# Both products of a squared-ReLU MLP by Strassen's seven products on halves, after a FoX attention layer

## The chip, the cores and the metric

The kernel runs on one core of a Trainium2 chip. The metric is the device time of one execution in microseconds (us): the median of several runs, 2275.89 us for the kernel before (three runs, 2275.84 to 2275.94). The profiled execution is another run of the same program.

## The reference

One decoder layer on 512 tokens (S) of width 2048 (D), all in float32. Attention has 16 heads of 128; the MLP is 8192 wide.

```python
h = rmsnorm(x, g[0])
proj = h @ w_in                                  # q, k, v and one forget gate per head
cum = cumsum(log_sigmoid(f_pre + b_f))           # per head
logits = q @ k.T * dh**-0.5 + cum[i] - cum[j]    # causal
h = softmax(logits) @ v @ w_out
x = x + rmsnorm(h, g[1])
h = square(relu(rmsnorm(x, g[2]) @ w1)) @ w2     # w1 [2048, 8192], w2 [8192, 2048]
x = x + rmsnorm(h, g[3])
```

## The kernel before

Every float32 operand is carried in two parts of TensorE's fp32r type: `h`, the value rounded by a cast on ScalarE (ACT), and `l`, the remainder, a subtraction on VectorE (DVE). `mm3` (L69 to L73) makes each product by three matmuls: h·h, h·l and l·h. A 512 KB block of weights comes by SyncE (SP) DMA into one of three `raw` buffers, ACT casts it (L65) and DVE subtracts (L66); four places of `whi` and `wlo` hold the blocks that TensorE (PE) works on.

The stages follow one another: values, queries and keys, per-head attention, output projection `py` in four chunks of 512 columns, first residual, MLP, last norm and residual. The output projection's last chunk goes by halves of the tokens (tiles 0, 1 and then 2, 3), so that the residual and the transposes of the first half (`turn_pair`) stand between PE's work on the second half, and those of the second half between PE's first MLP products (`first_chunk`, L520). All sixteen 256 KB tiles `xt` of the layer's input are loaded by GpSimd (POOL) well ahead (`load_x`, L412). `residual` (L440) scales the projected tile by the norm's factor and adds `xt`, for some tiles on POOL (L444, L445), for others on DVE (L447). The second norm's factor is a row `r2row` that is multiplied in after the first MLP product (L505), so nothing waits for it before PE starts.

The MLP goes in 16 chunks of four tiles of its width. `w1_chunk` makes four hidden tiles of 128 x 512 in PSUM, each over 16 tiles of D, with moving operands of 512 columns (the tokens); DVE takes the relu, ACT squares and casts, DVE makes the low part, and all stays in SBUF. `w2_chunk` of the chunk before follows: for each of four column chunks, four PSUM sums `po` of 128 tokens x 512 columns over the chunk's four hidden tiles, which DVE adds to sixteen accumulators `acc` in SBUF (L568). Chunks of the first and the second product alternate, so that each one's evacuation lies beside the other's matmuls. The last chunk's second product goes by tiles of tokens (`pz`, L609 to L640), each followed by its norm, residual and store.

Engines work in order, each through its own queue; an instruction that waits holds all behind it on that engine. The order is that of the code as a scheduler places it.

## Time and profile before

| what | value |
|---|---|
| median of three runs | 2275.89 us |
| profiled execution, first to last instruction (span) | 2273.5 us |
| PE busy, matmuls | 2257.2 us, 9978 |
| DVE, ACT, POOL busy | 1002.4, 667.5, 130.0 us |
| DMA, hardware queue and POOL's software queue | 226.65 MB and 6.33 MB |
| mean granted PE clock | 0.998 of 2.4 GHz |

Times are us from the span's start, durations of one instruction ns where so marked. A PE instruction's own duration overlaps its neighbours', because matmuls are pipelined: what one costs in a run of many is the distance from start to start, which the time-ordered view shows. "Idle before" is how long the engine stood still in front of the instructions of a row, with the instruction that ended most of it. A DMA row's last number is the median from issue to landing.

### The profile page before, as it was taken

What the parts mean: (1) busy time and instruction counts of PE and PEld (TensorE: products, weight loads), DVE (VectorE), ACT (ScalarE), POOL (GpSimd) and SP (SyncE); (2) the same over time, 40 slices, a digit from 0 to 9 for tenths busy, and PEclk for the clock granted to TensorE, in tenths of its full rate; (3) what the DMA queues carried; (4) which work ended last, traced back from release to release, by engine and by line L of the source; (5) the groups of instructions that cost most, each with busy time, mean ns of one, the idle gap of its engine ahead of it and who ended that gap; (6) DMA issues with size and microseconds to landing.
All of it is one profiled execution on the core that took longest, in us unless ns stands there. A gap on an engine that the chain in (4) does not pass through costs nothing.

```text
span 2273.5 us, 24519 instructions
## 1 busy us (share of the span) xinstructions
PE 2257.2 (99%) x9978; PEld 1826.0 (80%) x9978; DVE 1002.4 (44%) x1312; ACT 667.5 (29%) x981; POOL 130.0 (6%) x147
## 2 busy tenths in 40 slices
PE   9999999999999999999999999999999999999998
PEld 7788888888888888888888888888888888888886
DVE  9553452544542383433334334334334343343455
ACT  4433332333432363222222222222222222222232
POOL 8000000000010030000000000000000000000002
PEclk9999999999999999999999999999999999999999
DMA  5322222222243362222222222322222222322243
GB/s 173 117 90 86 92 88 93 88 89 92 85 153 116 122 211 94 93 93 98 95 95 93 93 93 93 94 96 96 94 93 93 93 94 94 98 95 93 93 146 123
DMA packets 70720, 234.55 MB, mean 103 GB/s; under 512 B 8128, under 2 KB 8512, under 8 KB 70352
## 3 DMA queue, kind: packets, MB, share of 16 engines
q1 hardware_dynamic: 68832, 226.65, 30.8%
q0 software_dynamic: 1632, 6.33, 0.8%
q8 instruction: 78, 1.28, 0.2%
q14 instruction: 34, 0.28, 0.0%
q10 hardware_dynamic: 144, 0.02, 0.0%
HBM read 224.54 MB, written 8.42 MB: 102 GB/s over the span
## 4 chain that ended last, share of the span: by engine, by line
PE 95%; DVE 3%; DMA 1%; issue 1%; ACT 1%; SPq 0%; DVEq 0%; ACTq 0%
PE ph L73 10%; PE ph L71 10%; PE ph L72 10%; PE po L72 10%; PE po L73 10%; PE po L71 10%; PE pk L71 3%; PE pk L72 3%; PE pq L72 3%; PE pq L73 3%; PE pk L73 3%; PE pq L71 3%; PE py L71 2%; PE py L73 2%; PE py L72 2%; PE pv L71 2%
## 5 line engine op out<-in xcount | busy, mean ns | idle before, releaser
L71 PE MATMUL ph<-acth,whi_a 128*128 128x512 f32 (+1 forms) x1056 | 412.1, 390 | 0.0
L72 PE MATMUL ph<-actl,whi_a 128*128 128x512 f32 (+1 forms) x1056 | 411.4, 390 | 0.0
L73 PE MATMUL ph<-acth,wlo_a 128*128 128x512 f32 (+1 forms) x1056 | 411.3, 390 | 0.0
L72 PE MATMUL po<-wlo_b,hh 128*128 128x512 f32 x960 | 379.3, 395 | 0.0
L71 PE MATMUL po<-whi_b,hh 128*128 128x512 f32 x960 | 379.2, 395 | 0.0
L73 PE MATMUL po<-whi_b,hl 128*128 128x512 f32 x960 | 379.2, 395 | 0.0
L65 ACT CAST whi_a<-raw_a 128x1024 fp32r<-128x1024 f32 x128 | 134.6, 1052 | 523.5 <-PE ph L72 268.5
L66 DVE TENSOR_TENSOR wlo_a<-raw_a,whi_a 128x1024 fp32r<-128x1024 f32 x128 | 157.2, 1228 | 265.0 <-ACT whi_a L65 264.8
L65 ACT CAST whi_b<-raw_b 128x1024 fp32r<-128x1024 f32 x120 | 126.0, 1050 | 496.0 <-PE po L73 257.6
L66 DVE TENSOR_TENSOR wlo_b<-raw_b,whi_b 128x1024 fp32r<-128x1024 f32 x120 | 147.1, 1225 | 253.1 <-ACT whi_b L65 253.1
L72 PEld LDWEIGHTS ph<-actl,whi_a 128*128 128x128 f32 x1056 | 199.0, 188 | 45.6
L73 PEld LDWEIGHTS ph<-acth,wlo_a 128*128 128x128 f32 x1056 | 199.0, 188 | 45.5
L71 PEld LDWEIGHTS ph<-acth,whi_a 128*128 128x128 f32 x1056 | 198.9, 188 | 45.4
L71 PEld LDWEIGHTS po<-whi_b,hh 128*128 128x128 f32 x960 | 180.0, 188 | 44.1
L72 PEld LDWEIGHTS po<-wlo_b,hh 128*128 128x128 f32 x960 | 180.0, 187 | 44.0
L73 PEld LDWEIGHTS po<-whi_b,hl 128*128 128x128 f32 x960 | 179.9, 187 | 44.0
L568 DVE TENSOR_TENSOR acc<-po,acc 128x512 f32<-128x512 f32 x224 | 149.3, 686 | 78.7 <-PE po L73 78.5
L505 DVE SCALAR_TENSOR_TENSOR a<-ph,r2row 128x512 f32<-128x512 f32 x64 | 44.2, 691 | 216.6 <-PE ph L73 216.5
L73 PE MATMUL pv<-whi_v,actl 128*128 128x512 f32 x256 | 102.0, 398 | 3.0 <-DVE actl L191 3.0
L72 PE MATMUL pv<-wlo_v,acth 128*128 128x512 f32 x256 | 102.2, 399 | 0.6 <-DVE wlo_v L66 0.2
L71 PE MATMUL pv<-whi_v,acth 128*128 128x512 f32 x256 | 102.4, 402 | 0.2 <-ACT whi_v L65 0.2
L71 PE MATMUL py<-whi_o,acth 128*128 128x512 f32 x256 | 102.6, 401 | 0.0
(171 smaller groups left out, 2868.1 us busy)
## 6 DMA issues: line engine op xcount, KB each, us to landing
raw_a<-in_w SPq DMA_DIRECT2D x128, 512.0 KB, 3.7
raw_b<-in_w SPq DMA_DIRECT2D x120, 512.0 KB, 3.5
raw_o<-in_wo SPq DMA_DIRECT2D x40, 512.0 KB, 3.5
raw_q<-in_wq SPq DMA_DIRECT2D x32, 512.0 KB, 3.7
raw_k<-in_wk SPq DMA_DIRECT2D x32, 512.0 KB, 3.8
raw_v<-in_wv SPq DMA_DIRECT2D x24, 512.0 KB, 3.5
xr<-in_xT SPq DMA_DIRECT2D x16, 256.0 KB, 4.0
raw_v<-in_wv SPq DMA_DIRECT2D x16, 256.0 KB, 4.1
```

The costliest lines, as they stand in the source:

```text
L65: nc.scalar.copy(hi[:, c], raw[:, c])
L66: nc.vector.tensor_tensor(out=lo[:, c], in0=raw[:, c], in1=f32(hi[:, c]), op=ALU.subtract)
L71: nc.tensor.matmul(o, a[0], b[0], start=start, stop=False)
L72: nc.tensor.matmul(o, a[0], b[1], start=False, stop=False)
L73: nc.tensor.matmul(o, a[1], b[0], start=False, stop=stop)
L505: nc.vector.scalar_tensor_tensor(out=a, in0=ps, scalar=0.0, in1=r2row, op0=ALU.max, op1=ALU.mult)
L568: nc.vector.tensor_tensor(out=acc[t, c], in0=po[t], in1=acc[t, c], op=ALU.add)
```

## The change

Seven products of quarter-size blocks replace eight in both MLP products, for 30 of the 32 pairs of hidden tiles. A pair is 256 hidden columns. In the first product the halves are of the inner dimension D, of the pair's hidden columns (128 and 128) and of the tokens (256 and 256); in the second they are of the pair's hidden tiles, of the tokens and of the 2048 output columns, taken 256 + 256 at a time in four column pairs `cp`. Every matmul of both now has 256 moving columns.

- Weights (`load_seven`): one SP DMA of 512 KB brings four blocks of 256 columns, DVE makes the four sums that the scheme needs (`t8_combine`), ACT casts the seven operands (1792 columns in one instruction), DVE subtracts (1792). There are two places for the split operands and three `raw` buffers.
- First product: the normed input's seven combinations are made once (`turn`, `mix`, `split_mix`) and stay in SBUF. The first 512 hidden columns are done plainly, by halves of the tokens (`plain`), while those are made. Then each pair is 168 matmuls into four PSUM banks; `evac_seven` combines the seven sums, takes relu and square, and POOL stores the hidden tile to DRAM (`hd`).
- Second product: `load_h` brings a pair back from DRAM by POOL's DMA, combines and splits it. Five chunks of six pairs; in each, four column pairs; in each of these, seven PSUM sums of 128 x 512 over six pairs. ACT copies the sums to four `st` buffers and POOL's DMA writes them to DRAM (`md`), plainly in the first chunk and with addition in the other four. The two MLP products no longer alternate.
- At the end `gather` reads `md` back and combines seven sums into four for each column pair; the last two pairs of hidden tiles are added as before (`pz`).
- The second norm's factor is now applied to the residual tiles (`norm2`) ahead of the transposes. The input tiles have two buffers for each half of the tokens' work, loaded by POOL inside `residual`. Head outputs go to DRAM and come back for the output projection (`od`).

```diff
@@ helpers in place of the [128, 1024] blocks of the MLP
+    AOF = [1, 6, 0, 4, 3, 5, 2]
+    def t8_combine(z):
+        nc.vector.tensor_tensor(out=z[:, 4:6], in0=z[:, 1:3], in1=z[:, 0:1].to_broadcast([P, 2, 256]), op=ALU.add)
+        nc.vector.scalar_tensor_tensor(out=z[:, 6], in0=z[:, 4], scalar=-1.0, in1=z[:, 2], op0=ALU.mult, op1=ALU.subtract)
+        nc.vector.tensor_tensor(out=z[:, 7], in0=z[:, 3], in1=z[:, 6], op=ALU.subtract)
+    def split7(z, at):
+        hi, lo = slots(at, 7), slots(at + SLOT, 7)
+        nc.scalar.copy(hi, z[:, 1:8])
+        nc.vector.tensor_tensor(out=lo, in0=z[:, 1:8], in1=f32(hi), op=ALU.subtract)
+        return hi, lo
+    def load_seven(src, name):
+        raw = raw_tile(f"raw_{name}").rearrange("p (n c) -> p n c", c=256)
+        nc.sync.dma_start(raw[:, 0:4], src)
+        t8_combine(raw)
+        tplace[0] += 1
+        return split7(raw, WBASE + tplace[0] % 2 * 2 * SLOT)
...
@@ residual, second norm, mixed inputs
-                y = vpool.tile([P, 512], F32, tag="yg", name=f"yg_{c}_{t}", bufs=16)
...
-            xx = mp.tile([P, 512], F32, tag="xt", name=f"xt_{c}_{t}", bufs=16)
...
+        def residual(hf, c, on_pool):
+            for t in halves[hf]:
+                xx = tr.tile([P, 512], F32, tag="xt", name=f"xt_{c}_{t}", bufs=2)
+                cs = slice(c * 512, (c + 1) * 512)
+                nc.gpsimd.dma_start(xx, x[t * P:(t + 1) * P, cs])
+                y, r = yg[t, c], r1[:, t:t + 1]
+                if on_pool:
+                    nc.gpsimd.tensor_scalar(out=y, in0=y, scalar1=r, scalar2=None, op0=ALU.mult)
+                    nc.gpsimd.tensor_tensor(out=y, in0=y, in1=xx, op=ALU.add)
+                else:
+                    nc.vector.scalar_tensor_tensor(out=y, in0=y, scalar=r, in1=xx, op0=ALU.mult, op1=ALU.add)
+                nc.sync.dma_start(x2d[:, t, cs], y)
+                nc.scalar.activation(xx, y, AF.Square, accum_out=ssx[:, t, c:c + 1])
+        def norm2(hf):
...
+            for c in (0, 2, 1, 3):
+                for t in halves[hf]:
+                    nc.scalar.activation(yg[t, c], yg[t, c], AF.Copy, scale=r2[:, t:t + 1])
+        def turn(hf, p):
...
+        def mix(p, x4):
...
+            nc.vector.tensor_tensor(out=x4[:, 0:512], in0=f32(opr[:, at:at + 512]), in1=f32(opr[:, at + 512:at + 1024]), op=ALU.add)
+            nc.vector.tensor_tensor(out=m[:, 0:2], in0=z[:, 1:3], in1=z[:, 3:4].to_broadcast([P, 2, 256]), op=ALU.subtract)
+            nc.vector.tensor_tensor(out=m[:, 2], in0=m[:, 1], in1=z[:, 1], op=ALU.add)
+            nc.vector.tensor_tensor(out=m[:, 3], in0=z[:, 0], in1=m[:, 2], op=ALU.subtract)
+            return m4
...
+        for hf in range(2):
+            for kb in range(8):
+                out_unit(py, NC - 1, kb, halves[hf])
+                if hf == 1:
+                    if kb == 0:
+                        norm1(0)
+                        for c in range(NC):
+                            residual(0, c, c % 2 == 1)
+                        norm2(0)
+                    if kb >= 6:
+                        for p in range(4 * kb - 24, 4 * kb - 20):
+                            turn(0, p)
+            evac_y(py, NC - 1, halves[hf])
...
+        def plain(hf, p):
+            w = load_split(w1p[p], f"a{hf}_{p}")
+            cols = slice(256 * hf, 256 * (hf + 1))
...
+        for p in range(8):
+            plain(0, p)
+            if p == 0:
+                norm1(1)
+                for c in range(NC):
+                    residual(1, c, c == 1)
+                norm2(1)
+        for p in range(8):
+            plain(1, p)
+            split_mix(p, m4[p])
+            if p + 2 < 8:
+                m4[p + 2] = mix(p + 2, x4[p + 2])
+            if p + 3 < 8:
+                x4[p + 3] = turn(1, p + 3)
@@ first product
-    def w1_tile(ci, f):
-        ps = psum_acc(f"ph_{ci}_{f}")
-        for hb in range(2):
-            w1_mm(ps, w1_block(ci, f, hb), hb)
-        return ps
...
+        def square(h4, src, n):
+            if src is not None:
+                nc.scalar.activation(h4, src, AF.Relu)
+            nc.scalar.activation(h4, h4, AF.Square)
+            nc.gpsimd.dma_start(hd[n], h4)
...
+        def evac_seven(b, n):
...
+            nc.scalar.copy(s1[:, 0], b[0][:, 0:256])
+            nc.vector.tensor_tensor(out=ev[:, 0:6:5], in0=two[1], in1=s1.to_broadcast([P, 2, 256]), op=ALU.add)
+            nc.vector.tensor_tensor(out=ev[:, 1], in0=b[2][:, 0:256], in1=ev[:, 0], op=ALU.add)
+            nc.vector.scalar_tensor_tensor(out=ev[:, 2:7:4], in0=two[0][:, 1:2].to_broadcast([P, 2, 256]), scalar=-1.0, in1=ev[:, 0:2],
+                                           op0=ALU.mult, op1=ALU.subtract)
+            nc.vector.tensor_tensor(out=ev[:, 3:5], in0=two[3], in1=ev[:, 1:3], op=ALU.add)
+            square(h4, ev[:, 3:7].rearrange("p n c -> p (n c)"), n)
+        for n in range(2, NPAIR):
+            b = [(psum_acc if n % 2 else psum_att)(f"ps_{n}_{i}") for i in range(4)]
+            for g in range(4):
+                w = load_seven(w1s[n - 2, g], f"a{n}_{g}")
+                for j in range(7):
+                    bi, part = WHERE[j]
+                    for kk in range(2):
+                        p = 2 * g + kk
+                        mm3b(b[bi][:, part * 256:(part + 1) * 256], [zz[:, j, kk * P:(kk + 1) * P] for zz in w], xop(p, AOF[j]),
+                             p == 0 and FIRST[bi] == j, p == 7)
+            evac_seven(b, n)
@@ second product
-    def w2_chunk(ci, hs):
...
-                    nc.vector.tensor_tensor(out=acc[t, c], in0=po[t], in1=acc[t, c], op=ALU.add)
...
+    def load_h(pool, n):
+        h8 = pool.tile([P, 8, 256], F32, tag="h8", name=f"h8_{n}", bufs=2)
+        nc.gpsimd.dma_start(h8[:, 0:4], hd[n].rearrange("p (n c) -> p n c", c=256))
+        nc.vector.tensor_tensor(out=h8[:, 4:6], in0=h8[:, 2:4], in1=h8[:, 0:1].to_broadcast([P, 2, 256]), op=ALU.subtract)
+        nc.vector.tensor_tensor(out=h8[:, 6], in0=h8[:, 5], in1=h8[:, 2], op=ALU.add)
+        nc.vector.tensor_tensor(out=h8[:, 7], in0=h8[:, 1], in1=h8[:, 6], op=ALU.subtract)
+        return split7(h8, n % NRING * 2 * SLOT)
...
+        for n in range(3):
+            want(n)
+        for ci in range(NCHUNK):
+            n0 = ci * CHUNK
+            for cp in range(4):
+                po = []
+                for k in range(CHUNK):
+                    n = n0 + k
+                    w = load_seven(w2s[n, cp], f"b{n}_{cp}")
+                    for j in range(7):
+                        if k == 0:
+                            po.append(psum(f"po_{ci}_{cp}_{j}"))
+                        for t in range(2):
+                            mm3b(po[j][:, t * 256:(t + 1) * 256], [zz[:, AOF[j], t * P:(t + 1) * P] for zz in hops[n]], [zz[:, j] for zz in w],
+                                 k == 0 and t == 0, k == CHUNK - 1)
+                    if ci == 0 and cp == 0 and k < 3:
+                        want(n + 3)
+                    elif ci > 0 and cp == 0 and k in (0, 2):
+                        want(n0 + 4 + k // 2)
+                    if cp in (1, 2) and k == 2:
+                        want(n0 + CHUNK + cp - 1)
+                    if cp == 3 and k in (2, 4):
+                        want(n0 + CHUNK + 1 + k // 2)
...
+                for j in range(7):
+                    st = w2pool.tile([P, 512], F32, tag="st", name=f"st_{ci}_{cp}_{j}", bufs=4)
+                    nc.scalar.copy(st, po[j])
+                    if ci == 0:
+                        nc.gpsimd.dma_start(md[cp, :, j], st)
+                    else:
+                        nc.gpsimd.dma_start(md[cp, :, j], st, accum_op=ALU.add)
...
@@ end
+        def gather(cp):
+            ma = raw_tile(f"ma_{cp}").rearrange("p (n c) -> p n c", c=512)
+            mb = raw_tile(f"mb_{cp}").rearrange("p (n c) -> p n c", c=512)
+            nc.sync.dma_start(ma, md[cp, :, 0:4])
+            nc.sync.dma_start(mb[:, 0:3], md[cp, :, 4:7])
...
+            nc.vector.tensor_tensor(out=p6, in0=p1, in1=p6, op=ALU.add)
+            nc.vector.tensor_tensor(out=y(0, 0), in0=two(p1), in1=two(p2), op=ALU.add)
+            nc.vector.tensor_tensor(out=p3, in0=p3, in1=p5, op=ALU.subtract)
+            nc.vector.tensor_tensor(out=y(0, 1), in0=two(p3), in1=two(p6), op=ALU.subtract)
+            nc.vector.tensor_tensor(out=p7, in0=p6, in1=p7, op=ALU.add)
+            nc.vector.tensor_tensor(out=y(1, 0), in0=two(p7), in1=two(p4), op=ALU.add)
+            nc.vector.scalar_tensor_tensor(out=y(1, 1), in0=two(p5), scalar=-1.0, in1=two(p7), op0=ALU.mult, op1=ALU.subtract)
```

In POOL's queue the first half's residual stood like this before: sixteen loads of the input far ahead, then only arithmetic (`yg` the projected tile, `xt` the input tile, `r1` the first norm's factor; names end in a running number).

```order
L415 DMA xt_3_0_5867<-in_x 128x512
L415 DMA xt_3_1_5869<-in_x 128x512
L415 DMA xt_3_2_5871<-in_x 128x512
L415 DMA xt_3_3_5873<-in_x 128x512
L444 TENSOR_SCALAR yg_2_0_5853<-yg_2_0_5853,r1_5875 128x512
L444 TENSOR_SCALAR yg_2_1_5857<-yg_2_1_5857,r1_5875 128x512
L445 TENSOR_TENSOR xt_2_0_5599<-yg_2_0_5853,xt_2_0_5599 128x512
L445 TENSOR_TENSOR xt_2_1_5601<-yg_2_1_5857,xt_2_1_5601 128x512
L444 TENSOR_SCALAR yg_3_0_6030<-yg_3_0_6030,r1_5875 128x512
L444 TENSOR_SCALAR yg_3_1_6034<-yg_3_1_6034,r1_5875 128x512
L445 TENSOR_TENSOR xt_3_0_5867<-yg_3_0_6030,xt_3_0_5867 128x512
L445 TENSOR_TENSOR xt_3_1_5869<-yg_3_1_6034,xt_3_1_5869 128x512
```

Now the loads stand among the arithmetic, each pair of buffers behind its last reader:

```order
L507 TENSOR_SCALAR yg_0_0_4960<-yg_0_0_4960,r1_4948 128x512
L507 TENSOR_SCALAR yg_1_0_4962<-yg_1_0_4962,r1_4948 128x512
L507 TENSOR_SCALAR yg_0_1_4961<-yg_0_1_4961,r1_4948 128x512
L507 TENSOR_SCALAR yg_1_1_4963<-yg_1_1_4963,r1_4948 128x512
L504 DMA xt_1_0_5625<-in_x 128x512
L504 DMA xt_1_1_5631<-in_x 128x512
L508 TENSOR_TENSOR yg_0_0_4960<-yg_0_0_4960,xt_1_0_5625 128x512
L504 DMA xt_2_0_5637<-in_x 128x512
L508 TENSOR_TENSOR yg_1_0_4962<-yg_1_0_4962,xt_1_1_5631 128x512
L504 DMA xt_2_1_5642<-in_x 128x512
L504 DMA xt_3_0_5647<-in_x 128x512
L508 TENSOR_TENSOR yg_0_1_4961<-yg_0_1_4961,xt_3_0_5647 128x512
```

All four scalings of the tiles done on POOL now come ahead of the third load, and each addition behind the load of its own tile.

On ACT, at the end of one column pair and the start of the next in the second product, before (chunk with `hs`, weights `whi_b`, then the next chunk's `whi_a`) there are casts of weights and the hidden tiles' squares only:

```order
L507 CAST hh_1_2_7018<-sqh_1_2_7017 128x512
L65 CAST whi_b0_1_0_7170<-raw_b0_1_0_7169 128x1024
L65 CAST whi_b0_1_1_7200<-raw_b0_1_1_7199 128x1024
L506 ACTIVATE sqh_1_3_7086<-a_1_3_7085 128x512
L507 CAST hh_1_3_7087<-sqh_1_3_7086 128x512
L65 CAST whi_b0_2_0_7242<-raw_b0_2_0_7241 128x1024
L65 CAST whi_b0_2_1_7272<-raw_b0_2_1_7271 128x1024
```

Now seven copies of sums stand between the casts (`raw_b6_2` is pair 6's weights for column pair 2; `po_1_1_3` the fourth sum of chunk 1, column pair 1):

```order
L434 CAST opr_69<-raw_b11_1_14828 128x1792
L434 CAST opr_69<-raw_b6_2_14898 128x1792
L750 COPY st_1_1_0_14877<-po_1_1_0_14576 128x512
L750 COPY st_1_1_1_14880<-po_1_1_1_14583 128x512
L750 COPY st_1_1_2_14883<-po_1_1_2_14590 128x512
L750 COPY st_1_1_3_14886<-po_1_1_3_14597 128x512
L750 COPY st_1_1_4_14889<-po_1_1_4_14604 128x512
L434 CAST opr_69<-raw_b7_2_14954 128x1792
L750 COPY st_1_1_5_14892<-po_1_1_5_14611 128x512
L750 COPY st_1_1_6_14895<-po_1_1_6_14618 128x512
L434 CAST opr_69<-raw_b8_2_15003 128x1792
```

Five copies are ahead of the cast of the next column pair's second operand; the fifth copy needs the `st` buffer of the first, free when that one's DMA has landed.

POOL's queue where the first product ends and the second starts is new: the store of the last hidden pair stands ahead of the load of the first (before, POOL has nothing to do between the second half's residual and the last chunk's `pz`; `hd` is the hidden layer in DRAM, `h4_31` the tile of pair 31, `h8_0` the buffer that pair 0 comes back to).

```order
L637 DMA hd_4951<-h4_29_12440 128x1024
L637 DMA hd_4951<-h4_30_12651 128x1024
L637 DMA hd_4951<-h4_31_12862 128x1024
L679 DMA h8_0_12875<-hd_4951 128x1024
L679 DMA h8_1_12882<-hd_4951 128x1024
L679 DMA h8_2_12889<-hd_4951 128x1024
L679 DMA h8_3_12952<-hd_4951 128x1024
```

The three loads that the second product starts from stand behind the store of pair 31.

## Rows read from the trace of the kernel before

**Rows 1.** The page: busy time of each engine, and the chain by engine.

```profile
PE 2257.2 (99%) x9978; PEld 1826.0 (80%) x9978; DVE 1002.4 (44%) x1312; ACT 667.5 (29%) x981; POOL 130.0 (6%) x147
...
PE 95%; DVE 3%; DMA 1%; issue 1%; ACT 1%; SPq 0%; DVEq 0%; ACTq 0%
```

**Rows 2.** Busy time by stretch: residual, MLP, last chunk, some `ph`, start; columns as headed.

```profile
core 0: us, PE busy (x) PEld busy (x) DVE busy (x) ACT busy (x) POOL busy (x), PEclk, DMA share, GB/s
797.00:860.00 63.00, 60.83 (x386) 53.88 (x385) 45.80 (x76) 37.17 (x85) 22.59 (x13) 1.00 0.59 198
860.00:2200.00 1340.00, 1340.00 (x5736) 1076.90 (x5736) 530.85 (x603) 328.42 (x372) 0.00 (x0) 1.00 0.29 94
2200.00:2273.50 73.50, 65.00 (x291) 52.69 (x289) 42.90 (x89) 19.59 (x50) 16.08 (x13) 0.97 0.44 154
...
842.00:850.00 8.00, 8.00 (x69) 7.96 (x67) 4.93 (x11) 4.68 (x11) 0.00 (x0) 1.00 0.32 90
...
23.00:25.00 2.00, 2.00 (x7) 1.52 (x6) 2.00 (x3) 0.20 (x1) 2.00 (x3) 0.50 0.74 260
```

**Rows 3.** PE in time: 512 columns (eight in a row, first and last).

```profile
817.66 0.40 PE L71 MATMUL py<-whi_o,acth 128*128 128x512 f32 x1
...
819.30 0.39 PE L72 MATMUL py<-wlo_o,acth 128*128 128x512 f32 x1
```

**Rows 4.** PE in time: 256 columns, 77 in a row in `ph`, 24 in `pz`.

```profile
838.96 0.28 PE L71 MATMUL ph<-acth,whi_a 128*128 128x256 f32 x1
...
848.08 0.28 PE L72 MATMUL ph<-actl,whi_a 128*128 128x256 f32 x1
...
2262.01 0.28 PE L71 MATMUL pz<-acth,hh 128*128 128x256 f32 x1
...
2264.72 0.28 PE L73 MATMUL pz<-acth,hl 128*128 128x256 f32 x1
```

**Rows 5.** DVE, groups by line, 797 to 2200 us.

```profile
L66 DVE TENSOR_TENSOR wlo_a<-raw_a,whi_a 128x1024 fp32r<-128x1024 f32 x128 | 157.2, 1228 | 265.0 <-ACT whi_a L65 264.8
L568 DVE TENSOR_TENSOR acc<-po,acc 128x512 f32<-128x512 f32 x216 | 143.8, 686 | 74.7 <-PE po L73 74.5
L463 DVE SCALAR_TENSOR_TENSOR actl<-xT,gc,acth 128x256 fp32r<-128x256 f32 x32 | 14.3, 478 | 3.9 <-ACT acth L462 3.7
L447 DVE SCALAR_TENSOR_TENSOR xt<-yg,r,xt 128x512 f32<-128x512 f32 x10 | 9.6, 1020 | 0.1
```

**Rows 6.** ACT, groups by line, 797 to 2200 us; the last, 70 to 660 us.

```profile
L65 ACT CAST whi_a<-raw_a 128x1024 fp32r<-128x1024 f32 x128 | 134.6, 1052 | 523.5 <-PE ph L72 268.5 <-PE po L73 254.9
L506 ACT ACTIVATE sqh<-a 128x512 f32<-128x512 f32 x64 | 40.5, 633 | 0.8 <-DVE a L505 0.8
L485 ACT ACTIVATE jx<-xt 128x512 f32<-128x512 f32 x16 | 10.3, 655 | 1.9 <-DVE xt L447 1.9
L485 ACT ACTIVATION_READ_ACCUMULATOR jx<-xt 128x1 f32 x16 | 3.5, 222 | 0.0
...
L331 ACT COPY o<-o 128x512 f32<-128x512 f32 x15 | 8.8, 588 | 7.2 <-PE o L329 7.2
```

**Rows 7.** POOL in time, first half's residual.

```profile
798.54 3.88 POOL L444 TENSOR_SCALAR yg<-yg,r 128x512 f32<-128x512 f32 x2 [117.75 <-DVE r L100]
802.39 4.21 POOL L445 TENSOR_TENSOR xt<-yg,xt 128x512 f32<-128x512 f32 x2
```

**Rows 8.** DMA issues: KB each, median us to landing.

```profile
raw_a<-in_w SPq DMA_DIRECT2D x128, 512.0 KB, 3.7
...
xt<-in_x POOLq DMA_DIRECT2D x16, 256.0 KB, 7.9
x2d<-xt SPq DMA_DIRECT2D x16, 256.0 KB, 3.6
...
g3b<-in_grow POOLq DMA_DIRECT2D x1, 1024.0 KB, 4.9
...
cumd<-cum POOLq DMA_DIRECT2D x1, 32.0 KB, 2.6
```

**Rows 9.** PE in time after a wait near the start.

```profile
21.96 0.50 PE L73 MATMUL pv<-whi_v,actl 128*128 128x512 f32 x1 [2.97 <-DVE actl L191]
...
22.85 0.63 PE L73 MATMUL pv<-whi_v,actl 128*128 128x512 f32 x1
...
25.41 0.63 PE L73 MATMUL pv<-whi_v,actl 128*128 128x512 f32 x1
```

**Rows 10.** DVE in time, the last instruction.

```profile
2267.61 2.46 DVE L637 SCALAR_TENSOR_TENSOR acc<-acc,r,x 128x256 f32<-128x256 f32 x4
```

More of the change, by code (lines that the diff above doesn't have):

```diff
@@ L25 @@
 NPLACE = KT + 2
+SLOT = 7 * 256
+NRING = 8
+WBASE = NRING * 2 * SLOT
+NCOL = WBASE + 4 * SLOT
+ABASE = NPLACE * 1024
+NPAIR = FT // 2
+NSTR = NPAIR - 2
+CHUNK = 6
 WARM = 9
@@ L368, in split_o @@
         def split_o(h):
+            o = ap_.tile([P, S], F32, tag="o32", name=f"o_{h}", bufs=4)
+            nc.sync.dma_start(o, od[h])
             ah, al = act_pair()
[L370 to L371 removed]
+            nc.scalar.copy(ah, o)
+            nc.vector.tensor_tensor(out=al, in0=o, in1=f32(ah), op=ALU.subtract)
             o_hl[h] = (ah, al)
@@ L465, in fox_layer @@
-    py = [psum_acc(f"py_{NC - 1}_{t}") for t in range(TT)]
-    pair = 0
-    for hf in range(2):
-        for kb in range(8):
-            out_unit(py, NC - 1, kb, halves[hf])
-            if hf == 1:
-                if kb == 0:
-                    norm1(0)
-                    for c in range(NC):
-                        residual(0, c, c >= 2)
-                while pair < 8 and kb >= 2 + pair * 6 // 8:
-                    turn_pair(0, pair)
-                    pair += 1
-        evac_y(py, NC - 1, halves[hf])
@@ new lines, in fox_layer @@
+    with ExitStack() as w1s_:
+        w1pool = w1s_.enter_context(tc.tile_pool(name="w1pool", bufs=2, reuse_waits="tile"))
+        def square(h4, src, n):
[3 more added lines that the diff above has]
+            nc.gpsimd.dma_start(hd[n], h4)
+        for n in range(2):
+            h4 = w1pool.tile([P, 1024], F32, tag="h4", name=f"h4_{n}")
+            for fh in range(2):
+                for hf, i in enumerate(((2, 0), (1, 3))[fh]):
+                    nc.scalar.activation(h4[:, i * 256:(i + 1) * 256], ph[2 * n + fh][:, hf * 256:(hf + 1) * 256], AF.Relu)
+            square(h4, None, n)
+        WHERE = [(0, 0), (3, 1), (1, 1), (0, 1), (2, 0), (1, 0), (3, 0)]
+        FIRST = {0: 0, 1: 2, 2: 4, 3: 1}
+        def evac_seven(b, n):
+            ev = w1pool.tile([P, 7, 256], F32, tag="ev", name=f"ev_{n}")
+            s1 = w1pool.tile([P, 1, 256], F32, tag="s1", name=f"s1_{n}")
+            h4 = w1pool.tile([P, 1024], F32, tag="h4", name=f"h4_{n}")
+            two = [z.rearrange("p (n c) -> p n c", c=256) for z in b]
+            nc.scalar.copy(s1[:, 0], b[0][:, 0:256])
[16 more added lines that the diff above has]
+            evac_seven(b, n)
@@ new lines, in fox_layer, with last_w @@
+    NCHUNK = NSTR // CHUNK
+    hops = {}
+    bank[0] = 4
+    wlast, hlast = {}, {}
+    def last_w(i):
+        raw = raw_tile(f"raw_z{i}")
+        nc.sync.dma_start(raw[:, 0:1024], w2p[i // 2, i % 2])
+        hi, lo = opr[:, i * 2048:i * 2048 + 1024], opr[:, i * 2048 + 1024:i * 2048 + 2048]
+        nc.scalar.copy(hi, raw[:, 0:1024])
+        nc.vector.tensor_tensor(out=lo, in0=raw[:, 0:1024], in1=f32(hi), op=ALU.subtract)
+        for kk in range(2):
+            wlast[i // 2, 2 * (i % 2) + kk] = [z[:, kk * 512:(kk + 1) * 512] for z in (hi, lo)]
@@ new lines, in fox_layer, with last_h, want @@
+    with ExitStack() as w2s_:
+        w2pool = w2s_.enter_context(tc.tile_pool(name="w2pool", bufs=2, reuse_waits="tile"))
+        def last_h(i):
+            n = NSTR + i
+            raw = w2pool.tile([P, 2048], F32, tag="h8", name=f"hz_{i}", bufs=2)
+            nc.gpsimd.dma_start(raw[:, 0:1024], hd[n])
+            at = 6 * 2 * SLOT + i * 2048
+            hi, lo = opr[:, at:at + 1024], opr[:, at + 1024:at + 2048]
+            nc.scalar.copy(hi, raw[:, 0:1024])
+            nc.vector.tensor_tensor(out=lo, in0=raw[:, 0:1024], in1=f32(hi), op=ALU.subtract)
+            for fh in range(2):
+                for hf, m in enumerate(((2, 0), (1, 3))[fh]):
+                    hlast[2 * i + fh, hf] = [z[:, m * 256:(m + 1) * 256] for z in (hi, lo)]
+        def want(n):
+            if n < NSTR:
+                hops[n] = load_h(w2pool, n)
+        for n in range(3):
[21 more added lines that the diff above has]
+                        want(n0 + CHUNK + 1 + k // 2)
+                    if ci == NCHUNK - 1:
+                        if cp in (1, 2) and k == 2:
+                            last_h(cp - 1)
+                        if cp == 3 and k > 0:
+                            for i in range((k - 1) * 8 // 5, k * 8 // 5):
+                                last_w(i)
+                for j in range(7):
[3 more added lines that the diff above has]
+                        nc.gpsimd.dma_start(md[cp, :, j], st)
+                    else:
+                        nc.gpsimd.dma_start(md[cp, :, j], st, accum_op=ALU.add)
```

387 lines of the change are left out of this document (176 added, 211 removed).

## The prediction, made before the changed kernel ran

> **What bounds the kernel now.** I read the page first: PE is busy 99% of the span and the chain that ended last is PE for 95% of it; no other engine is above 44% [rows 1]. The busy time by stretch then shows where PE is not full: between 860 and 2200 us it never stops, 1340.00 of 1340, while DVE works 40% and ACT 25% of that stretch; around the residual it misses 2.17 us of 63, and in the last 73.5 us 8.5 [rows 2]. PE's time order gives the price of a matmul in a stream, which is the distance between starts, not the duration in the row. With 512 columns it is (819.30 − 817.66) / 7 = 0.234 us [rows 3]; 5736 matmuls in 1340 us give 0.2336 as well, so that I take 0.2335 for all of them. With 256 columns it is 9.12 / 76 = 0.1200 us in `ph` and 2.71 / 23 = 0.1178 in `pz` [rows 4]; I take 0.1195, nearer to the longer stretch. So the kernel is bound by the number of columns that pass through PE, and the change is judged by how many it saves and by how long PE then waits for operands.
>
> **What PE saves.** Before, the first product has 192 matmuls of 256 columns and 2976 of 512, the second 2880 of 512, and the last chunk 180 of 512 and 24 of 256: 216 × 0.1195 + 6036 × 0.2335 = 1435 us. After, there are 384 plain ones, 30 × 168 in the first product and 30 × 4 × 42 in the second, all of 256 columns, and the same last 204: 10,464 × 0.1195 + 180 × 0.2335 + 24 × 0.1195 = 1295 us. The saving is 140 us; at 0.1178 it would be 157, at 0.1200 it would be 134. The break-even price of a short matmul is 0.1195 + 140 / 10,464 = 0.1329 us if nothing else were lost.
>
> In the two stretches of rows 4 a matmul with half the columns costs 0.51 of a long one. The Trainium skill (TensorE: Matmul & The Clock Gate, section Back-to-back issue gap) speaks against such a trade: it gives a stream of weight load and matmul pairs 131 ns at 512 columns and 81 ns at 128, by which an estimate for 256, on the line between, is 98 ns or 0.75 of the long one. By that page the change would lose about 250 us; the trace disagrees at both lengths, with 0.234 and 0.120 us.
>
> **What the other engines must now deliver.** A DVE subtraction of 1024 columns takes 1.228 us and an addition of 512 takes 0.686 [rows 5]: 1.06 ns a column and 0.14 us fixed, so 2.04 us for 1792, 0.41 for 256. One block of seven is then 0.69 + 0.48 (the row of 478 ns for two inputs and a scalar) + 0.41 + 2.04 = 3.6 us; started back to back they overlap a little. A pair of the first product costs DVE 4 × 3.6 + 2.5 for the sevens' sums = 17 us, one of the second 4 × 3.6 + 3.6 for the hidden pair = 18 us, against 168 × 0.1195 = 20.1 us of PE. DVE goes from 40% to 84 to 90%: not the bound, but with two operand places and queues in order any hitch reaches PE. ACT's cast of 1792 columns, by 1.052 us for 1024 and 0.633 for 512 [rows 6], is 1.7 us; ACT is at half load. For small slips in the first product I take 6 us over 30 pairs (bounds 0 and 30, the latter one cast of about 1 us late in each pair).
>
> **The residual, where PE will wait longest.** Before, the input tiles were there and PE had transposes and half-token products to fill the time. Now, in the first half, POOL first does four scalings, 7.8 us by the rate of 3.88 for two [rows 7]; then each pair of tiles is load, addition, ACT's square, and only then the next load of that buffer. A load costs between 2.6 us (32 KB alone on that queue) and 7.9 (sixteen in a bunch) [rows 8]; for two in flight I take 4. With 2.1 us for POOL's addition or 1.02 for DVE's [rows 5, 7], and 0.88 for the square and its sum [rows 6], a pair of tiles takes about 6.5 us and four of them 26. The squares sit in ACT's queue ahead of the casts of the last output weights, so PE's second half of the output projection (96 matmuls, 22 us) is held too. With factor, norm (8 scalings of 0.65 = 5.2 us) and eight transposes the plain products of the first half begin some 50 us after the first half's sums are done, not 22. The second half repeats this beside 23 us of plain products, and then `plain(1, p)` runs at DVE's pace: `turn`, `mix` and `split_mix` for one p are about 5.3 us of DVE against 2.9 of PE. From the first half's sums to the first Strassen product that is 50 + about 28 (the second half's residual, as long as the first's behind the factor, of which 23 us lie beside the plain products) + 6 + 8 × 5.3 = 126 us, of which PE works 22 + 7 (transposes) + 46 = 75. That is 51 us of waiting against 2 before [rows 2]: +49. Bounds: 25 if loads take 2.6 and the halves overlap, 80 if they take 7.9.
>
> **The turn from the first to the second product.** Before, chunks alternate, and hidden tiles never leave SBUF. Now PE stops at the last sum of pair 31 and waits for sums and copies (4 us), relu and square of 1024 columns (1.05 each), the store (0.5 issue and 3.6 as `x2d` [rows 8]), the load of pair 0, which stands behind that store in POOL's queue (0.5 and about 4), its combination (1.5) and cast (1.7): 18 us, and 5 to 6 more until low parts and following pairs have caught up. I take +24, bounds 12 (load not held by the store) and 33 (both at 7.9).
>
> **Chunk boundaries and sums to DRAM.** At each of four chunk changes four new hidden pairs must be split on a DVE that is 90% full while their ring places come free only late; their subtractions and casts are 4 × 3.6 us of extra work in one column pair of 30. I take 5 us each, +20, bounds 0 and 32. At the end of every column pair ACT copies seven sums, 0.59 each [rows 6], to four buffers. The first sum is done 6 × 0.717 = 4.3 us ahead of the last; the fifth copy waits until the first has landed (X after its copy); behind it on ACT stands the cast of the next operand, with DVE's subtraction behind that, wanted 42 × 0.1195 = 5.0 us into the next column pair. PE waits for X − (4.3 + 5.0 − 0.59 − 0.59 − 1.7 − 2.04) = X − 4.4. An addition into DRAM is in no row. Bounds: 2.6 and 3.6 (small load of POOL, a plain store) give nothing; 7.9 gives 3.5 us at each of 16 ends, 56 us; a load and a store in line, 7.9 + 3.6, give 7.1 and 114. A load of 1 MB alone on POOL's queue takes 4.9 [rows 8], and with that as the nearest row, only one DMA being in flight in front of the fifth copy, X − 4.4 = 0.5 and the term is 8 us.
>
> The Trainium skill (DMA: Bandwidth & Descriptors, section Anatomy of one DMA — SWDGE) gives a plain transfer of this queue 2.0 us and its bytes at 436 GB/s; an estimate for 256 KB by that page is 2.6 us, by which this term would be nothing and the residual would stand at its lower bound, 24 us less. The `cumd` row of 2.6 agrees, the sixteen loads at 7.9 do not.
>
> **The small rest.** After a wait of 2.97 us PE's granted clock was 0.50, its lower level of 1.2 GHz, and matmuls stood 0.43 apart instead of 0.23 from 22.85 to 25.41, seven times 0.2 or 1.4 us [rows 2, 9]; I take +5 for some waits of this length, bounds 0 and 12. At the end the gathered sums of `md` come through a DRAM round trip and 28 DVE additions of 0.69; the last DVE instruction ends at 2270.07 now [rows 10], and I give the end +4 and the head outputs' way through DRAM +3 (bounds −2 and +20 together).
>
> **Sum.** −140 + 49 + 6 + 24 + 20 + 8 + 5 + 7 = −21. The profiled span of 2273.5 becomes 2252.5; the median of the runs lies 2.4 above that span, so I predict **2255 us**.
>
> **Rivals.**
> *The waits are mostly covered* (chance 0.30). For it: DVE and ACT were idle for most of the time at every one of these places before [rows 2], and I have laid steps end to end that may overlap. Against it: both residual halves need the whole row's sum of squares before any transpose. With 25, 2, 14, 8, 0, 2 and 3 for the terms the sum is −140 + 54 = −86, and the time about 2190.
> *The additions into DRAM are slow* (0.17). Place: the fifth `st` copy at sixteen column-pair ends, with ACT's casts behind it. X = 7.9 gives 56 us in place of the 8, 2303; X = 11.5 gives 114, 2361. It decides from X = 6.2, where 16 × 1.8 = 29 us take what is left of the saving. For it: the only bunched POOL transfers of the trace take 7.9. Against it: other single ones take 2.6 and 4.9.
> *Short matmuls don't hold 0.1195 for 1200 us* (0.08). PE's weight loads fill the 256-column stretches where they fill 80% of the long ones [rows 2]; at 0.125 the change loses 58 us of its saving: 2313. Against it: 77 in a row beside a busy DVE.
> That the change does not do what it says is excluded by the order: 10,464 short matmuls stand in PE's queue.
>
> **How the numbers follow.** My forecast has 0.45, with a range of its own of 2225 to 2285 (the terms of the residual and of the chunk boundaries at half way to their bounds). Below the first rival's 2190 I leave 0.10, above 2315 another 0.10: the range is 2185 to 2315. No change is what lies within 0.2% or 4.6 us of the median. Faster: all of the first rival and 0.35 of the 0.45, 0.65. Same: 0.06, from the forecast. Slower: 0.04 from the forecast and the other two rivals, 0.29.
>
> **What will show it.** Right: PE starts in the Strassen products 0.118 to 0.120 apart; no PE idle inside a pair; one gap of about 50 to 60 us in all around the residual, one of about 18 at the turn with the chain through `hd`, and `st` copies that wait at most 1 us for the accumulating DMA. Wrong: `md` additions landing after 6 us or more; DVE above 95% over a pair with PE waiting on the low parts; spacing above 0.122; or a residual of less than 30 us of waiting, which would put the time near 2200.

## The result, and the profile after

The changed kernel takes 2307.27 us (four runs, 2300.1 to 2310.08) against 2275.86 of the kernel before on the same chip: 1.0134 times, interval 1.0119 to 1.0150. It is slower by 1.3%; I had forecast 2255 and faster. The time lies inside my range, on the side of the rivals. The four runs of the changed kernel span 10 us (the longer ones at the lower mean granted clock, 0.966 against 0.973), those of the kernel before 0.1 us, so gains of a few us between variants of the changed kernel stay uncertain.

The page of the profiled execution, span 2305.3, answers to [rows 1]:

```profile
PE 2150.9 (93%) x14386; PEld 1992.7 (86%) x14386; DVE 1509.2 (65%) x1969; ACT 968.8 (42%) x1157; POOL 281.0 (12%) x354
...
issue 46%; PE 36%; DMA 6%; DVE 5%; POOL 5%; ACT 2%; POOLq 0%; SPq 0%; DVEq 0%; ACTq 0%
```

PE's busy time fell by 106 us, so the saving came, but the span has 154 us in which PE does nothing, where it had 16. The chain puts 46% down to "issue", which names no cause; the stages and the waits are read instead. The busy time by stretch (columns as in [rows 2]: residual, first product, turn, second product, end, and four microseconds inside the second product):

```profile
797.00:920.00 123.00, 76.80 (x495) 71.01 (x496) 76.15 (x122) 71.07 (x129) 19.46 (x22) 0.81 0.46 148
920.00:1530.00 610.00, 602.26 (x5019) 602.06 (x5018) 482.42 (x604) 271.30 (x210) 15.99 (x30) 1.00 0.40 131
1530.00:1560.00 30.00, 19.64 (x146) 19.38 (x147) 20.67 (x25) 11.63 (x7) 3.18 (x6) 0.77 0.43 146
1560.00:2240.00 680.00, 623.93 (x4919) 614.96 (x4918) 491.34 (x576) 315.00 (x288) 125.05 (x163) 0.96 0.66 170
2240.00:2305.00 65.00, 40.81 (x182) 33.28 (x180) 50.52 (x91) 14.26 (x41) 22.62 (x17) 0.84 0.74 245
1714.00:1718.00 4.00, 4.00 (x22) 4.00 (x22) 1.82 (x3) 2.27 (x2) 1.72 (x2) 0.57 1.09 261
```

The first product runs full at full clock. The second, with the same 5040 matmuls, needs 698 us (first matmul 1539.86, last 2237.4) where the first needed 607. PE's waits, each with the instruction that ended them (total, times, longest):

```profile
PE po L453 <- ACT st L750: 30.0, 16, 2.8
PE xT L528 <- ACT yg L521: 24.5, 2, 14.8
PE po L453 <- ACT opr L434: 23.3, 6, 17.6
PE po L454 <- DVE opr L435: 19.2, 9, 4.6
PE ph L95 <- DVE opr L88: 10.1, 5, 4.3
```

Fifteen of the sixteen waits for `st` (28.7 us) follow column pairs whose sums are added in DRAM; the first, 1.3 us, lies in chunk 0. One of the fifteen on ACT, in time order (start, duration, idle before; the copies of the third and fourth sum, then the fifth, a cast, the sixth):

```profile
1704.47 1.09 ACT L750 COPY st<-po 128x512 f32<-128x512 f32 x2
1708.83 0.59 ACT L750 COPY st<-po 128x512 f32<-128x512 f32 x1 [3.27 <-DMA md<-st]
1709.31 1.69 ACT L434 CAST opr<-raw_b 128x1792 fp32r<-128x1792 f32 x1
1713.17 0.59 ACT L750 COPY st<-po 128x512 f32<-128x512 f32 x1 [2.17 <-DMA md<-st]
```

and what PE does at its end:

```profile
1713.81 0.39 PE L453 MATMUL po<-opr 128*128 128x256 f32 x1 [2.61 <-ACT st L750]
...
1714.38 0.38 PE L454 MATMUL po<-opr 128*128 128x256 f32 x1
...
1717.76 0.32 PE L455 MATMUL po<-opr 128*128 128x256 f32 x1
```

The fifth copy waits for the DMA of the first, the sixth for that of the second, and PE waits 2.61 us for the bank that the sixth empties: the program rotates eight banks, so the seventh sum of a column pair goes where the sixth of the pair before was. All fifteen waits stand there, 36 matmuls into the next column pair. The first and the second store of this bunch (KB, us from issue to landing):

```profile
md<-st POOLq DMA_DIRECT2D x1, 256.0 KB, 4.3
```

```profile
md<-st POOLq DMA_DIRECT2D x1, 256.0 KB, 8.1
```

Over the sixteen adding bunches the seven stores land, in their order, after 4.3, 7.4, 8.2, 9.0, 6.6, 6.4 and 6.4 us (medians). From 1714.38 on PE's matmuls stand 0.21 apart for 3.4 us, at 0.57 granted clock over four microseconds. The landing of all stores (KB each, median us), chunk 0 with plain stores, 1560 to 1690, then the adding chunks, 1690 to 2240:

```profile
md<-st POOLq DMA_DIRECT2D x28, 256.0 KB, 4.6
```

```profile
md<-st POOLq DMA_DIRECT2D x109, 256.0 KB, 7.1
```

### The profile page after: what moved, and what is told of

Read it like the earlier page. It is cut to its first block, busy times and chain, and to the rows that moved or that the text cites. A ratio compares the mean times of both kernels' runs of the same rounds, so it can differ in the third digit from the quotient of the medians.

```text
span 2305.3 us, 34783 instructions
## 1 busy us (share of the span) xinstructions
PE 2150.9 (93%) x14386; PEld 1992.7 (86%) x14386; DVE 1509.2 (65%) x1969; ACT 968.8 (42%) x1157; POOL 281.0 (12%) x354
## 4 chain that ended last, share of the span: by engine, by line
issue 46%; PE 36%; DMA 6%; DVE 5%; POOL 5%; ACT 2%; POOLq 0%; SPq 0%; DVEq 0%; ACTq 0%
POOL md L754 3%; PE pq L95 3%; PE pk L95 3%; PE pk L93 3%; PE pq L94 3%; PE pk L94 3%; PE pq L93 3%; PE py L93 2%; PE py L95 2%; PE py L94 2%; DMA md<-st 2%; PE pv L94 2%; PE pv L95 2%; PE pv L93 2%; DMA xt<-in_x 2%
## 5 line engine op out<-in xcount | busy, mean ns | idle before, releaser
L453 PE MATMUL po<-opr 128*128 128x256 f32 x1680 | 472.6, 290 | 53.4 <-ACT st L750 30.0
L454 PE MATMUL po<-opr 128*128 128x256 f32 x1680 | 485.6, 291 | 19.3 <-DVE opr L435 19.2
L455 PE MATMUL po<-opr 128*128 128x256 f32 x1680 | 481.0, 290 | 1.4 <-DVE opr L435 1.4
L453 PE MATMUL ps<-opr 128*128 128x256 f32 x1680 | 476.2, 283 | 4.5 <-ACT opr L434 4.5
L454 PE MATMUL ps<-opr 128*128 128x256 f32 x1680 | 476.1, 283 | 0.0
L455 PE MATMUL ps<-opr 128*128 128x256 f32 x1680 | 475.5, 283 | 0.2 <-DVE opr L435 0.2
L453 PEld LDWEIGHTS po<-opr 128*128 128x128 f32 x1680 | 325.7, 197 | 58.5 <-ACT st L750 33.7
L454 PEld LDWEIGHTS po<-opr 128*128 128x128 f32 x1680 | 334.3, 199 | 22.4 <-DVE opr L435 21.8
L455 PEld LDWEIGHTS po<-opr 128*128 128x128 f32 x1680 | 332.9, 199 | 1.9 <-DVE opr L435 1.8
L435 DVE TENSOR_TENSOR opr<-raw_b,opr 128x1792 fp32r<-128x1792 f32 x120 | 242.8, 2023 | 134.5 <-ACT opr L434 134.1
L453 PEld LDWEIGHTS ps<-opr 128*128 128x128 f32 x1680 | 323.1, 192 | 4.7 <-ACT opr L434 4.7
L454 PEld LDWEIGHTS ps<-opr 128*128 128x128 f32 x1680 | 323.2, 192 | 0.0
L455 PEld LDWEIGHTS ps<-opr 128*128 128x128 f32 x1680 | 322.8, 192 | 0.5 <-DVE opr L435 0.5
L435 DVE TENSOR_TENSOR opr<-raw_a,opr 128x1792 fp32r<-128x1792 f32 x120 | 243.0, 2025 | 113.6 <-ACT opr L434 113.6
L434 ACT CAST opr<-raw_b 128x1792 fp32r<-128x1792 f32 x120 | 202.5, 1689 | 262.9 <-PE po L455 196.2
L434 ACT CAST opr<-raw_a 128x1792 fp32r<-128x1792 f32 x120 | 202.2, 1685 | 215.7 <-PE ps L454 199.8
L93 PE MATMUL py<-opr 128*128 128x512 f32 x256 | 101.2, 395 | 6.3 <-ACT opr L87 3.8
L95 PE MATMUL pv<-opr 128*128 128x512 f32 x256 | 100.6, 393 | 3.0 <-DVE opr L214 3.0
```

The lines of the kernel that those rows point to most:

```text
L93: nc.tensor.matmul(o, a[0], b[0], start=start, stop=False)
L95: nc.tensor.matmul(o, a[1], b[0], start=False, stop=stop)
L434: nc.scalar.copy(hi, z[:, 1:8])
L435: nc.vector.tensor_tensor(out=lo, in0=z[:, 1:8], in1=f32(hi), op=ALU.subtract)
L453: nc.tensor.matmul(o, a[0], b[0], start=start, stop=False, skip_group_check=True)
L454: nc.tensor.matmul(o, a[0], b[1], start=False, stop=False, skip_group_check=True)
```

## The experiments

Each was timed beside the kernel before (medians of 2275.77, 2275.95 and 2276.26 in the three groups).

**Eight `st` buffers** (`bufs=4` to `bufs=8`).

> Eight st buffers in place of four, nothing else. Theory A (the fifth copy of a sum waits for the first one's accumulating DMA to land, 7.1 us in the changed kernel, and each such PE wait is followed by some 3.4 us at half clock): the 30.0 us in which PE waits for st fall under 3, most of the 16 or so half-clock stretches in the second product go too (another 20 us), and the end gains some 5 because the last sums leave earlier: 2250 to 2260 against 2307. Rival B (VectorE at 85 to 90% load is the bound of the second product, and the st waits only stand in front of its waits): PE's waits move to opr from VectorE, 2295 to 2307. Rival C (the additions' extra DMA traffic slows the weight loads): no change of PE's waits for operands, and what is gained is the 30 us at most, 2277.

2299.55 us, 1.0104 (1.0087 to 1.0120). The `st` waits are gone as theory A had it, but the gain is 8 us, no more than the spread of the runs, and not 50. The time lies in rival B's range and PE's waits did move to VectorE, but not for B's reason, VectorE's load: VectorE itself waits for the weights. Here PE's longest wait, VectorE's first sum of a weight block from 1560 to 2230 us in this run, and the same group in the changed kernel:

```profile
PE po L454 <- DVE opr L435: 44.7, 29, 4.6
```

```profile
L427 DVE TENSOR_TENSOR raw_b<-raw_b 128x512 f32<-128x512 f32 x115 | 79.0, 688 | 105.7 <-DMA raw_b<-in_w2s 105.2
```

```profile
L427 DVE TENSOR_TENSOR raw_b<-raw_b 128x512 f32<-128x512 f32 x114 | 78.2, 687 | 32.1 <-DMA raw_b<-in_w2s 31.7
```

The idle time in front of it, ended by the weights' DMA, went from 32 to 106 us; the adding DMAs, all seven issued within 6.2 us, land after 9.0 us (median from 1690 to 2200). Of some 90 weight loads after 1690, 22 take more than 6 us to land, where it was 13 in the changed kernel. With four buffers the copies held the adding DMAs back; with eight they hold the weights. Buffers moved the wait.

**Plain stores in all chunks.**

```diff
-                        nc.gpsimd.dma_start(md[cp, :, j], st, accum_op=ALU.add)
+                        nc.gpsimd.dma_start(md[cp, :, j], st)
```

> The sums of chunks 1 to 4 are written over the old ones instead of being added to them (the addition is left out), four st buffers as in the changed kernel. Theory A: landing falls from 7.1 us to about 4.6 (the plain writes of chunk 0), at which the formula X - 4.4 gives 0.2 us at a column pair's end: PE's waits for st 0 to 5 us in all, 2255 to 2265. Rival B: 2295 to 2307. Rival C: as A here, but not in the run with eight buffers.

2257.37 us, 0.9919 (0.9904 to 0.9934): 50 us less than the changed kernel, with the same bytes and buffers. The `st` wait and the landing:

```profile
PE po L453 <- ACT st L750: 1.6, 2, 1.4
```

```profile
md<-st POOLq DMA_DIRECT2D x140, 256.0 KB, 4.6
```

Here is POOL's queue in the second product (packets, MB, share of 16 engines' time), of the changed kernel from 1712 to 2195 and of this one:

```profile
q0 software_dynamic: 16244, 33.76, 38.2%
```

```profile
q0 software_dynamic: 10329, 34.70, 20.5%
```

For as many MB the additions take the DMA engines almost twice as long. Only 2 of the weight loads after 1690 take more than 6 us now, and POOL issues a store in 0.54 us where an adding one takes 0.87. That settles it: the 50 us are the addition in the DMA, by the copies' buffers where these are few and by the weight loads where they are many. Of the 50, 46 lie in the second product: 31 are PE's waits, 9 the half clock, and most of the rest the matmuls right behind a wait, which are slower too.

**Additions on POOL.** POOL loads the old sum (four buffers), adds it to `st` (eight) and stores plainly.

```diff
+                        old = [fetch_m(ci, cp, j) for j in range(4)]
...
+                    if ci > 0:
+                        nc.gpsimd.tensor_tensor(out=st, in0=st, in1=old[j], op=ALU.add)
+                    nc.gpsimd.dma_start(md[cp, :, j], st)
```

> The additions of chunks 1 to 4 are done by POOL on SBUF tiles (the old sums loaded by plain DMA ahead, four buffers, eight st buffers) and stored plainly; no DMA adds. Theory C (in the run with eight buffers the seven adding DMAs in flight landed after 9 us and held the weight loads, so it is the adding DMA itself that costs the 50 us that the plain store gave back): 2257 to 2275. Theory F: POOL's additions lengthen VectorE's instructions beside them, at 88% load VectorE becomes the bound, 2285 to 2310.

2368.54 us, 1.0401 (1.0378 to 1.0424): theory F, and worse than it said. The subtraction of VectorE from 1700 to 2280 us, 2023 ns in the changed kernel, and PE's wait for it:

```profile
L435 DVE TENSOR_TENSOR opr<-raw_b,opr 128x1792 fp32r<-128x1792 f32 x91 | 222.2, 2442 | 47.1 <-ACT opr L434 46.8
```

```profile
PE po L454 <- DVE opr L435: 81.3, 31, 9.9
```

The mean hides two kinds: of these 91 subtractions the 53 with no addition of POOL beside them take 2.01 to 2.03 us each, while 17 of the others take 3.1 to 5.4 us. One of them:

```profile
1719.56 5.36 DVE L435 TENSOR_TENSOR opr<-raw_b,opr 128x1792 fp32r<-128x1792 f32 x1
```

So POOL's additions on SBUF lengthen VectorE's subtractions beside them, as the row of 1020 ns in [rows 5], beside POOL's scalings, had hinted. VectorE has no room for that here, so adding in the DMA was the better of the two.

**The first half's residual on VectorE** (`residual(0, c, c % 2 == 1)` to `residual(0, c, False)`).

> The first half's residual all on VectorE; POOL's four scalings (785.24 to 793.95 in the changed kernel), which stand ahead of the third load of the input, are gone. My step on the residual: the first half's chain starts 8 us sooner and PE's wait of 14.85 us ahead of the first transposes falls to 7 to 9, 2299 to 2302 against 2307. Rival: the chain of loads through two buffers sets the pace whatever the arithmetic, the wait stays at 12 or more, 2305 to 2308.

2289.96 us, 1.0059 (1.0044 to 1.0074): 17 us less, more than the 5 to 8 I expected, and by another way. The wait ahead of the first half's transposes is 11.63 where it was 14.85, nearer to the rival's 12 than to my 7 to 9: the loads through two buffers still set much of the pace. These transposes start 8 us sooner all the same: of two waits in the output projection one of 3.85 us is gone and one of 1.53 is now 1.35:

```profile
802.67 0.50 PE L94 MATMUL py<-opr 128*128 128x512 f32 x1 [1.35 <-DVE opr L88]
817.09 3.86 PE L528 MATMUL xT<-ident,yg 128*128 128x128 f32 x16 [11.63 <-ACT yg L521]
```

The rest comes from the second half. POOL's scaling there starts at 815.43, in the changed kernel at 839.32, and PE's wait ahead of the second half's transposes falls to 0.28 us (first row) from 9.68 in the changed kernel (second row):

```profile
852.77 2.14 PE L528 MATMUL xT<-ident,yg 128*128 128x128 f32 x16 [0.28 <-ACT yg L521]
```

```profile
870.99 4.45 PE L528 MATMUL xT<-ident,yg 128*128 128x128 f32 x20 [9.68 <-ACT yg L521]
```

The first Strassen matmul (the first of the two start times) comes at 897.9, in the changed kernel at 915.4:

```profile
L453 PE MATMUL ps<-opr x1680: 278/283/583, 897.9 to 1505.4; 128*128 128x256 f32 x187
```

```profile
L453 PE MATMUL ps<-opr x1680: 282/283/415, 915.4 to 1521.7; 128*128 128x256 f32 x187
```

All 17 us are won ahead of the first Strassen product, 8 in the first half and the rest in the second.

**Pairs 0 and 1 fetched ahead of the turn.** Their buffers get a place of their own, and the loads, sums and splits stand ahead of pair 31's sums.

```diff
...
+            if n == NPAIR - 1:
+                first = [fetch_h(m) for m in range(2)]
+                hops[0] = split7(first[0], 0)
             evac_seven(b, n)
+        hops[1] = split7(first[1], 2 * SLOT)
...
```

> The buffers of the hidden pairs lie beside those of the first product instead of in the same place, and pairs 0 and 1 are loaded, combined and split while pair 31's products run; the rest as in the changed kernel. My step on the turn: the 17.6 us wait and the few behind it fall to 2 to 6, 2288 to 2294 against 2307. Rival: the last sums of pair 31 still hold PE's banks and VectorE, 10 us of the wait stay, 2300.

2292.96 us, 1.0075 (1.0052 to 1.0099). This is within what I expected. The 17.6 us wait is gone (the longest of its kind is 3.2 us), and 14 us of time with it; the four runs span 13 us.

**The kernel before with its operands elsewhere.** In the changed kernel matmuls of 512 columns stand 0.227 us apart in the attention, in the kernel before 0.2335 [rows 3]. The edits move tiles only:

```diff
@@ kernel before, first and last of the four runs
+    acth = cpool.tile([P, NPLACE, 512], F32R, name="acth")
+    actl = cpool.tile([P, NPLACE, 512], F32R, name="actl")
     ones = cpool.tile([P, P], F32, name="ones")
...
-    acth = cpool.tile([P, NPLACE, 512], F32R, name="acth")
-    actl = cpool.tile([P, NPLACE, 512], F32R, name="actl")
@@ kernel before, third and last
-    bft = cpool.tile([H, 1], F32, name="bft")
+    bft = cpool.tile([H, 16], F32, name="bft")[:, 0:1]
@@ changed kernel, second run: opr 32 bytes further on
+    bft = cpool.tile([H, 1], F32, name="bft")
     opr = cpool.tile([P, NCOL], F32R, name="opr")
...
-    bft = cpool.tile([H, 1], F32, name="bft")
```

> The kernel before with acth and actl allocated first in their pool, so that they start at a multiple of 64 bytes instead of 32 bytes past one; nothing else. It is to tell why matmuls of 512 columns stand 0.2266 us apart in the attention of the changed kernel and 0.2334 in the kernel before. Theory D (the place of the operands): 0.2266 wherever acth or actl is an operand; if only the moving operand counts, in q, k and the first MLP product (about 4500 matmuls, 30 us, 2245), if both count also in v and the output projection (2232), while the second MLP product, whose stationary operands stay 32 bytes off, keeps 0.2334 or also falls. Rival E (it is the semaphores or the code around the matmuls): 0.2334 everywhere, 2276.

> The changed kernel with its one operand tensor moved by 32 bytes, so that every fp32r operand starts 32 bytes past a multiple of 64. Theory D: matmuls of 512 columns go from 0.2266 to 0.2334 (about 3200 of them, 20 us), those of 256 columns from 0.1200 to between 0.1200 and 0.1234 (0 to 35 us): 2327 to 2362. Rival E: no change, 2307.

> The kernel before with 64 bytes in place of 32 for the smallest tile, so that acth, actl and all tiles behind them, hh and hl too, start at multiples of 64 bytes. Theory D in the form that the last runs left (a matmul of 512 columns takes 0.2267 us where the stationary and the moving operand stand alike against 64 bytes, 0.2334 where they don't): the second product's 2880 and the last chunk's 180 fall too, 20 us less than with acth and actl alone, 2214 to 2218. Rival: only the first kind of operand counted, 2235.

> The kernel before with both edits: acth and actl first, and 64 bytes for the smallest tile, so that acth, actl, whi, wlo, hh and hl all start at multiples of 128 bytes. By the starts against 128 bytes the runs so far read: 0.2266 to 0.2274 us a matmul of 512 columns where moving and stationary operand have the same remainder (0 and 0, 32 and 32), 0.2289 to 0.2342 where they differ (32 and 0, 64 and 0, 0 and 64, 0 and 96). Theory D in this form: all 9000 matmuls at 0.227, 2235 less 3060 x 0.0066 = 20, 2213 to 2218. Rival: the two edits cancel in some other way, 2235 to 2247.

| kernel | start in bytes, remainder by 128: `acth`/`whi`/`hh` | `ph` | `py` | `po` | us |
|---|---|---|---|---|---|
| before | 32 / 0 / 96 | 0.2342 | 0.2333 | 0.2334 | 2275.86 |
| `acth` first | 0 / 0 / 96 | 0.2266 | 0.2267 | 0.2333 | 2235.19 |
| 64 bytes for `bft` | 64 / 0 / 0 | 0.2334 | 0.2289 | 0.2268 | 2246.95 |
| both edits | 0 / 0 / 0 | 0.2267 | 0.2267 | 0.2266 | 2214.21 |
| changed, shifted | all 32 | | 0.2269 | | 2309.07 |

(`ph`, `py`, `po`: mean distance in us from start to start, over some 380 to 610 matmuls of 512 columns; start bytes by the programs' allocations.) In the kernel with `acth` first, 41 matmuls in a row of each product:

```profile
1179.64 0.39 PE L73 MATMUL po<-whi_b,hl 128*128 128x512 f32 x1
...
1188.98 0.39 PE L71 MATMUL po<-whi_b,hh 128*128 128x512 f32 x1
...
1209.02 0.39 PE L73 MATMUL ph<-acth,wlo_a 128*128 128x512 f32 x1
...
1218.09 0.39 PE L71 MATMUL ph<-acth,whi_a 128*128 128x512 f32 x1
```

9.34 / 40 = 0.2335 and 9.07 / 40 = 0.2268. My first form of theory D, multiples of 64 bytes, fell: the third run came at 2246.95 where I had foretold 2214 to 2218, and the shifted kernel did not change. The form that held is that the two operands of a matmul start alike against 128 bytes. Foretold so, the last run came at 2214.21, 0.9729 (0.9715 to 0.9743): the fastest of all, with the arithmetic of the kernel before.

**Three mends at once** (eight buffers, fetching ahead, residual on VectorE).

> The changed kernel with three mends at once: eight st buffers, pairs 0 and 1 loaded ahead of the turn, the first half's residual all on VectorE; the adding DMAs stay. If the three places are apart, as the stages say, their gains add: 2307 less 8, 14 and 17 is 2268, just below the kernel before. Rival: they share the waits (the half-clock stretches, VectorE's queue at the start of the second product), 2275 to 2285.

2265.54 us, 0.9961 (0.9947 to 0.9975). The gains add (42 us, foretold 39), and the scheme then beats the kernel it replaced by 0.4%, but not that kernel with its operands moved.

## Why the prediction was wrong

By stages, each between instructions of the trace, with my terms gathered for it (122 is 126 less 4 us of norm factor; 641 is 602 + 6 + 20 + 8 + 5, 58 is 45 + 9 + 4; together 2248.5, 4 less than my sum by differences):

| stage | foretold, us | measured, us |
|---|---|---|
| to POOL's first scaling, 798.54 before [rows 7] | 801.5 | 785.24 |
| to the first Strassen product | 122 | 130.2 |
| first product | 608 | 606.7 |
| wait at the turn | 18 | 17.6 |
| second product | 641 | 697.6 |
| end | 58 | 67.8 |

**The saving** was right: 256 columns cost 0.120 in a stream over 5040 matmuls, and DVE at 79% (482.42 of 610) kept up. In the first product, 85 distances in 10.20 us:

```profile
999.75 0.28 PE L453 MATMUL ps<-opr 128*128 128x256 f32 x1
...
1009.95 0.28 PE L454 MATMUL ps<-opr 128*128 128x256 f32 x1
```

The rival of short matmuls that don't hold their price is out. So is the estimate by the Trainium skill (TensorE: Matmul & The Clock Gate, Back-to-back issue gap) of 0.75 of the long price: it is 0.51 to 0.53 in these traces. (The loss of about 250 us put beside it, an estimate too, comes to 236 by the page's two figures.)

**The step that failed is the addition into DRAM**, the term of 8 us at the column-pair ends, in its path and in what it does to the other transfers. I let the fifth copy wait for the first store, landing X after its copy, and PE wait X − 4.4 for the operand that ACT casts behind that copy. The first store does land after 4.3 us, not above the 4.9 I took; by my formula nothing would have been lost. What I left out is the sixth copy. It waits for the second store, which lands after 7.4 us, and PE needs the bank that it empties 36 matmuls into the next column pair, ahead of the operand at 42. That cost 30.0 us in sixteen waits of at most 2.8. The formula with the median of all seven stores, 7.1, gives 2.7 at each end and 43 in all, but that is not the path. Seven stores are issued within some 10 us, each taking about twice the engine time of a plain one. So the rival with a chance of 0.17 is what happened, though not at the fifth copy where it stood and for 30 us in place of its 56. That its 2303 is near 2307 is luck: the clock, the end and the attention below err by as much, in opposite ways. I also took buffers for the place of the cost; it is the DMA engines' time, which eight buffers only pass on to the weights.

The estimate by the Trainium skill (DMA: Bandwidth & Descriptors, Anatomy of one DMA — SWDGE) of 2.6 us for one such DMA is near what the first of a bunch takes when it is plain (2.3 us in the run of plain stores, chunks 1 to 4). It does not describe seven: 4.6 when plain, 7.1 when adding.

**The clock** was taken at 5 us in all. Over 1560 to 2240 the granted clock is 0.96: some 55 of the 680 us are at half clock, after about half of the waits for `st` and after the longer ones for VectorE. PE's matmuls stand 0.21 apart there instead of 0.12, in stretches of 3.4 or 6.8 us, which costs 24 us. I had priced one such stretch [rows 9] and not counted how many waits I was adding. The plain stores raise the clock from 1710 to 2200 from 0.96 to 0.98.

So the second product's 697.6 us are 605 of matmuls at 0.120, 30.0 of waits for `st`, 26.3 of other waits, 24 of half clock, 8 in the first matmul or so behind each wait, which I had put at nothing, and some 5 that I can't place.

**Terms that were near in size:** the turn (its whole 17.6 us went when pairs 0 and 1 were fetched and split ahead of it) and the chunk boundaries with the small slips (26 foretold, 20.6 for VectorE and 5.7 for ACT). The residual took 8 us more than foretold. Its loads landed after 5.3 us (median of fourteen) where I took 4; the lower bound of 2.6 was no load, since `cumd` lies in DRAM and that row is a store. POOL's scalings lasted 8.7 us (7.8 foretold), but 17 us came back without them, since the second half then starts earlier too. Why the end took 10 us more I did not trace.

**An error that hid part of the miss:** the attention and output projection came 13 us sooner although I had added 3 for them. In the changed kernel one tensor `opr` holds all operands, which therefore start alike; the kernel before with `acth` moved first reaches the same place at 780.22, 18 us sooner than unmoved. On kernels that are equal in this, the change costs more: 2307 against 2214.
